# Transposing query rows of two heads as fp32 and splitting them while they leave PSUM

## The chip, the cores and the metric

The kernel runs on one core of one Trainium2 chip. The metric is the device time of one execution in microseconds (us). Five engines matter here: TensorE (PE in the profile; its weight loads are PEld), VectorE (DVE), ScalarE (ACT), GpSimd (POOL) and SyncE (SP), the last two mainly as issuers of DMA transfers.

## The reference, cut to what matters

A decoder trunk of four layers on a sequence of 256 positions with 2048 features, all in fp32. Layers 0 and 3 are latent attention, layer 1 is attention with a selection of keys, layer 2 is attention in a window. Every layer has one input projection, four heads of attention to a memory, a SiLU gate and one output projection. Two places of it concern the change:

```python
# latent attention (layers 0 and 3): 16 heads, a plain part of 128 and a rotary part of 64
q_nope, q_rope = q[..., :A_NOPE], _rope(q[..., A_NOPE:])
s = (einsum('bqhd,bkhd->bhqk', qn, k_nope) + einsum('bqhd,bkd->bhqk', qr, k_rope)) * scale
...
# attention with the selection (layer 1): 32 heads of 64, 4 key heads
q = q.reshape(B, S, B_KV_HEADS, G, B_HEAD_DIM)
s = einsum('bqgjd,bqkgd->bqgjk', qb, kg) * B_HEAD_DIM ** -0.5 + bias
```

## The kernel before, in words

**Precision by two parts.** A product of fp32 accuracy is made from fp32r operands: a value v is split into a high part (v written as fp32r) and a low part (v minus the high part). `split` (lines 67 to 69) does this with a copy on ACT and a subtraction on DVE. The weights are split so, 512 columns at a time, into `wh` and `wl` (`parts_of`, line 234, three buffers of each); then TensorE multiplies high by high, high by low and low by high. `rows_by` (line 240) gives the product with positions on the partitions, `columns_by` (line 270) with features on the partitions; `gate` (line 460) is made of two `columns_by` of 16 steps each.

**Queries of 64 features.** A head with 64 features leaves half of the 128 contraction rows unused, so high and low part are stacked: 64 rows hold the high part and 64 the low part, and the key side holds the same key part in both halves. One pass over the stacked query then gives both products. Which half holds which part doesn't matter, since the key side is the same in both.

**How the stack is made before.** The product has positions on the partitions and must be transposed.
- Rotary queries (`rotary`, line 669; called from `project` for groups 0 and 2 of each latent layer, so four times): for two tiles `t` of 128 positions and two sets `z` of four heads, `rope` (line 592, four DVE instructions) writes `qrr`; `split` (line 678) writes high and low part side by side into `qrs`, of which there is one buffer; `transposed` (line 449) makes four 128x128 transposes in fp32r (line 456), one for each head, into one PSUM tile `tr`, and one ACT copy of 512 columns (line 457, recorded at line 60) into `self.qr`.
- Queries of layers 1 and 2 (`Grouped.project`, line 900; called for four groups in each): `stacked` (line 782) does the same from the accumulator, with an ACT copy that scales (line 787) and a DVE operation that scales and subtracts (line 788), then `transposed`.

So a head is transposed as one 128x128 tile that is half high part and half low part, for each of the two tiles of positions.

**What sets the order.** The kernel is written with a framework that orders each engine's instructions itself from its own estimate of their times (`schedule_with_timeline_sim=True`, line 1201); only what is passed to `keep_in_program_order` stays as written. An engine takes its instructions in that order. While a group's queries are made, the gate of the same group, the attention of the part before and its output projection (`w_out`, line 1113) are at hand for TensorE. PSUM has two kinds of buffers: four "acc" for projections, four "mp" for all else (scores, transposes, attention outputs).

**The order of heads in attention.** In layers 1 and 2 it is 0, 2, 1, 3, 4, 6, 5, 7 (line 917); the first four lie in the tile `q[0]`, the last four in `q[1]`. In latent layers it is 0 to 3 (line 707), all in one tile of `self.qr`.

Of the kernel before, what the change touches and what calls it, by code (L numbers as in the profile page):

```python
# [8 lines left out]
F32 = mybir.dt.float32  # L9
F32R = mybir.dt.float32r  # L10
# [5 lines left out]
P = 128  # L16
S = 256
# [6 lines left out]
A_QL, A_KVL, A_ROPE, A_NOPE = 1536, 512, 64, 128  # L24
# [7 lines left out]
def kernel(ctx: ExitStack, tc: tile.TileContext, a: dict, out: bass.AP,  # L32
                             kinds=(0, 1, 2, 0)):
    nc = tc.nc
# [4 lines left out]
    wk = ctx.enter_context(tc.tile_pool(name="wk", bufs=1))  # L39
# [3 lines left out]
    def misc(name, dt=F32):  # L43
        return ps.tile([P, 512], dt, name=name, tag="mp", bufs=4)
# [8 lines left out]
    def f32(ap):  # L53
        return ap.bitcast(F32)

    def part_tile(dt=F32R):
        return wk.tile([P, 512], dt, name="hl", tag="hl", bufs=2)

    def copy_act(o, i, scale=1.0):
        inst = nc.scalar.activation(o, i, AF.Copy, scale=scale)  # L60
        if pinned:
            tc.keep_in_program_order(inst)
# [4 lines left out]
    def split(hi, lo, src):  # L67
        copy_act(hi, src)
        nc.vector.tensor_sub(lo, src, f32(hi))  # L69
# [22 lines left out]
    ident = cst.tile([P, P], F32, name="ident")  # L92
# [147 lines left out]
    def rows_by(xt, kts, w, k0, cols, name, prepare=None, each=None, late=None):  # L240


        acc = [ps.tile([P, 512], F32, name=f"acc_{name}{t}", tag="acc", bufs=4) for t in range(2)]
        for s in range(0, kts, ST):
            m = min(ST, kts - s)
            wr, n = stage(w, k0 + s, m, cols, each)
            other_work()
            for k in range(m):
                if prepare is not None:
                    prepare(s + k)  # L250
                wh, wl = parts_of(wr, k * n, n)
                q = xt[(s + k) // 4]
                for t in range(2):
                    xh, xl = (q[:, v, (s + k) % 4, t * P:(t + 1) * P] for v in range(2))
                    first, last = s + k == 0, s + k == kts - 1
                    if late is not None and t == 0:

                        both = late[:, s + k].rearrange("p v c -> p (v c)")
                        if not last:
                            nc.tensor.matmul(acc[t][:, :n], both, wh[:, :n], start=first, stop=False)  # L260
                        nc.tensor.matmul(acc[t][:64, :n], both[:, :64], wl[:, :n], start=False, stop=False)
                        if last:
                            nc.tensor.matmul(acc[t][:, :n], both, wh[:, :n], start=False, stop=True)
                        continue
                    nc.tensor.matmul(acc[t][:, :n], xh, wh[:, :n], start=first, stop=False)  # L265
                    nc.tensor.matmul(acc[t][:, :n], xh, wl[:, :n], start=False, stop=False)  # L266
                    nc.tensor.matmul(acc[t][:, :n], xl, wh[:, :n], start=False, stop=last)  # L267
        return acc

    def columns_by(xt, kts, w, k0, cols, name):  # L270

        acc = [ps.tile([P, 2, S], F32, name=f"acc_{name}{j}", tag="acc", bufs=4) for j in range(2)]
        for s in range(0, kts, 2 * ST):
            m = min(2 * ST, kts - s)
            wr, n = stage(w, k0 + s, m, cols)
            other_work()
            for k2 in range(0, m, 2):
                wh, wl = parts_of(wr, k2 * S, 2 * S)
                for k in range(2):
                    kt = s + k2 + k  # L280
                    q = xt[kt // 4]

                    for j in range(2):
                        o = k * S + j * P
                        nc.tensor.matmul(acc[j], wh[:, o:o + P], q[:, :, kt % 4, :],  # L285
                                         start=kt == 0, stop=False)
                    for j in range(2):
                        o = k * S + j * P
                        nc.tensor.matmul(acc[j][:, 0, :], wl[:, o:o + P], q[:, 0, kt % 4, :],  # L289
                                         start=False, stop=kt == kts - 1)  # L290
        return acc

    def total(acc, name="z"):
        z = wk.tile([P, S], F32, name=name, tag="z", bufs=3)
        copy_act(z, acc[:, 1, :])
        nc.vector.tensor_add(z, z, acc[:, 0, :])
        return z
# [151 lines left out]
    def transposed(dst, srcs, c0=0):  # L449


        for i0 in range(0, len(srcs), 4):
            i1 = min(len(srcs), i0 + 4)
            tp = misc("tr", F32R)
            for i in range(i0, i1):
                nc.tensor.transpose(tp[:, (i - i0) * P:(i - i0 + 1) * P], srcs[i], identr)
            copy_act(dst(i0, i1), f32(tp)[:, :(i1 - i0) * P].rearrange("p (j c) -> p j c", c=P)[:, :, c0:])


    def gate(nm, w, c0):  # L460
        gT = act.tile([P, 4, S], F32, name="gT", tag="gT", bufs=2)
        for h in range(2):
            acc = columns_by(nm.at, 16, w, 0, (c0 + h * S, S), "g")
            for j in range(2):
                z = total(acc[j])
                hz = wk.tile([P, S], F32, name="hz", tag="z", bufs=3)
                nc.vector.tensor_mul(hz, z, nm.half)
                th = wk.tile([P, S], F32, name="th", tag="e", bufs=4)
                nc.scalar.activation(th, hz, AF.Tanh)
                nc.vector.scalar_tensor_tensor(gT[:, 2 * h + j, :], th, 1.0, hz, op0=OP.add, op1=OP.mult)  # L470
        return gT
# [120 lines left out]
    def rope(dst, src, t, n):  # L592

        cb = cos[:, t, None, :].to_broadcast([P, n, A_ROPE])
        q = A_ROPE // 2
        rot = wk.tile([P, 4, A_ROPE], F32, name="rot", tag="rot", bufs=1)[:, :n]
        nc.vector.tensor_mul(rot[:, :, :q], src[:, :, q:], sin[:, t, None, :q].to_broadcast([P, n, q]))
        nc.vector.tensor_mul(rot[:, :, q:], src[:, :, :q], sin[:, t, None, q:].to_broadcast([P, n, q]))
        nc.vector.tensor_mul(dst, src, cb)
        nc.vector.tensor_add(dst, dst, rot)  # L600


    class Latent:
# [65 lines left out]
        def rotary(self, g):  # L669

            self.qr = [act.tile([P, 4, S], F32R, name="qrT", tag="aux", bufs=AUX) for z in range(2)]
            acc = rows_by(self.cT[:3], 12, a["w_uq"][self.j], 0, (g * 768, 8, 192, A_NOPE, A_ROPE), "qr")
            for t in range(2):
                for z in range(2):
                    rr = wk.tile([P, 4, A_ROPE], F32, name="qrr", tag="z", bufs=3)
                    rope(rr, acc[t][:, z * S:(z + 1) * S].rearrange("p (h d) -> p h d", h=4), t, 4)
                    rs = wk.tile([P, 4, 2, A_ROPE], F32R, name="qrs", tag="qrs", bufs=1)
                    split(rs[:, :, 0, :], rs[:, :, 1, :], rr)
                    transposed(lambda i0, i1: self.qr[z][:, i0:i1, t * P:(t + 1) * P],
                               [rs[:, h].rearrange("p a b -> p (a b)") for h in range(4)])  # L680

        def project(self, g):

# [50 lines left out]
    class Grouped:  # L734
# [165 lines left out]
        def project(self, g):  # L900
            nm = self.nm
            acc = rows_by(nm.at, 16, self.w, 0, (g * 512, 512), "q")
            q = [act.tile([P, 4, S], F32R, name="qS", tag="pq", bufs=PQ) for z in range(2)]
            for t in range(2):
                self.stacked(lambda i0, i1: q[i0 // 4][:, :, t * P:(t + 1) * P], acc[t],
                             nm.col("eighth", t), 8)
            bm = act.tile([P, 8, S], F32, name="bm", tag="big3")
            tab = tabs[0 if self.sparse else 1][g]
            nc.gpsimd.dma_start(bm, bass.AP(tensor=tab.tensor, offset=tab.offset + 127,
                                            ap=[[8 * N_TAB - 1, P], [N_TAB, 8], [1, S]]))  # L910
            return g, q, bm, gate(nm, self.w, self.g0 + g * 512)
# [189 lines left out]
    nm = Norm(0)  # L1101
# [3 lines left out]
    for i in range(depth):  # L1105
# [33 lines left out]
        else:  # L1139
            w_out(*pending, True)  # L1140
            nxt.finish()
            nm = nxt
# [62 lines left out]
```

## Time and profile before

| | before |
|---|---|
| median of three runs | 2587.08 us (2586.99 to 2587.45) |
| profiled execution | 2586.98 us |
| span in the profile, first to last instruction | 2585.2 us |
| mean granted TensorE clock | 0.999 |
| DMA, over the span | 520.02 MB, mean 201 GB/s |

How to read the rows below. A row of the waits says which engine, line and tile waited for which, with the total in us, the number of times and the longest. A row of the groups has the line, the engine, the operation, output and inputs with their shapes, the count; then busy us and the mean ns of one; then the idle time ahead of it on its engine and what ended it. A row of the timeline has the start and the length in us, the engine, the line and the count of like instructions in a row; a bracket gives idle time and what ended it. Copies and splits are recorded at lines 60 and 69, inside the helpers, so the tiles' names tell them apart: `tr` is the PSUM tile of a transpose, `qrT` the stacked rotary query, `qS` the stacked query of layers 1 and 2, `hl` the pair of parts of `stacked`, `ptp` the transposed attention weights, `x` at line 184 the rows of the residual stream.

### The profile page before, as it was taken

How to read it: one execution, taken by the hardware profiler on the slowest of the kernel's cores; microseconds unless marked ns; L12 is line 12 of the kernel's file. 1: busy time of each engine (PE TensorE's matmuls, PEld its weight loads, DVE VectorE, ACT ScalarE, POOL GpSimd, SP SyncE). 2: the span in 40 equal slices, each digit the busy share in tenths (PEclk: the TensorE clock that was granted, in tenths of full speed). 3: DMA queues.
4: the chain of work that ended last, by engine and by line, in shares of the span. 5: the costliest groups of instructions: out<-in, count | busy, mean ns of one | idle time of the engine just before them, and what ended most of it. 6: DMA issues, size and time to landing. Idle time of an engine off the chain costs nothing. (4 is left out here: it accounts for less than half of the span.)

```text
span 2585.2 us, 41767 instructions
## 1 busy us (share of the span) xinstructions
PE 2573.5 (100%) x14050; PEld 2214.7 (86%) x14050; DVE 1878.4 (73%) x4139; ACT 1622.3 (63%) x3451; POOL 86.8 (3%) x159
## 2 busy tenths in 40 slices
PE   9999999999999999999999999999999999999998
PEld 7888898888888888888888888888888888888887
DVE  6666667676776686877778776777778767777676
ACT  6556556556656566667666666676666655665655
POOL 1000000000000010000000000000000000000000
PEclk9999999999999999999999999999999999999999
DMA  9888777666777667566556575555655877676664
GB/s 305 257 256 268 236 219 229 184 167 195 190 203 202 196 216 247 167 203 189 187 166 199 169 225 171 172 174 185 195 156 147 240 203 198 192 195 180 212 172 179
DMA packets 459417, 520.02 MB, mean 201 GB/s; under 512 B 69521, under 2 KB 353057, under 8 KB 457537
## 3 DMA queue, kind: packets, MB, share of 16 engines
q1 hardware_dynamic: 441744, 449.72, 58.5%
q0 software_dynamic: 16736, 66.65, 8.0%
q8 instruction: 110, 1.80, 0.3%
q14 instruction: 107, 0.87, 0.1%
q10 hardware_dynamic: 720, 0.98, 0.1%
HBM read 494.10 MB, written 35.75 MB: 205 GB/s over the span
## 5 line engine op out<-in xcount | busy, mean ns | idle before, releaser
L69 DVE TENSOR_TENSOR wl<-wr,wh 128x512 fp32r<-128x512 f32 (+2 forms) x1720 | 1161.3, 678 | 619.0 <-ACT wh L60 597.2
L60 ACT ACTIVATE wh<-wr 128x512 fp32r<-128x512 f32 (+2 forms) x1720 | 1066.1, 621 | 800.5 <-PE acc_g L285 170.5
L285 PE MATMUL acc_g<-xT,wh 128*128 128x512 f32 x1536 | 486.7, 396 | 0.0
L289 PEld LDWEIGHTS acc_g<-xT,wl 128*128 128x128 f32 x1536 | 284.5, 188 | 60.5
L289 PE MATMUL acc_g<-xT,wl 128*128 128x256 f32 x1536 | 310.2, 280 | 0.0
L266 PE MATMUL acc_wo<-wl,y 128*128 128x512 f32 x752 | 297.3, 395 | 0.2 <-DVE wl L69 0.2
L267 PE MATMUL acc_wo<-wh,y 128*128 128x512 f32 x752 | 291.8, 390 | 0.0
L285 PEld LDWEIGHTS acc_g<-xT,wh 128*128 128x128 f32 x1536 | 238.3, 189 | 4.5
L265 PE MATMUL acc_wo<-wh,y 128*128 128x512 f32 x752 | 235.7, 392 | 0.2
L266 PEld LDWEIGHTS acc_wo<-wl,y 128*128 128x128 f32 x752 | 141.3, 188 | 27.7 <-DVE wl L69 0.6
L267 PEld LDWEIGHTS acc_wo<-wh,y 128*128 128x128 f32 x752 | 141.3, 188 | 27.3
L265 PEld LDWEIGHTS acc_wo<-wh,y 128*128 128x128 f32 x752 | 139.3, 188 | 28.7 <-ACT y L60 1.0
L285 PE MATMUL acc_mk<-mT,wh 128*128 128x512 f32 x512 | 161.5, 396 | 0.3 <-ACT wh L60 0.3
L285 PE MATMUL acc_mq<-xT,wh 128*128 128x512 f32 x512 | 161.6, 396 | 0.0
L1118 DVE TENSOR_TENSOR x<-x,acc_wo 128x512 f32<-128x512 f32 x184 | 121.1, 682 | 4.4 <-PE acc_wo L267 4.3
L285 PE MATMUL acc_qn<-cT,wh 128*128 128x512 f32 x384 | 121.3, 397 | 0.0
L285 PE MATMUL acc_cq<-xT,wh 128*128 128x512 f32 x384 | 120.9, 396 | 0.0
L289 PEld LDWEIGHTS acc_mk<-mT,wl 128*128 128x128 f32 x512 | 96.1, 188 | 22.8 <-DVE wl L69 0.4
L289 PEld LDWEIGHTS acc_mq<-xT,wl 128*128 128x128 f32 x512 | 93.9, 188 | 20.1
L289 PE MATMUL acc_mq<-xT,wl 128*128 128x256 f32 x512 | 103.1, 282 | 0.0
L266 PE MATMUL acc_q<-wl,xT 128*128 128x512 f32 x256 | 101.2, 395 | 0.0
L289 PE MATMUL acc_mk<-mT,wl 128*128 128x256 f32 x512 | 101.1, 278 | 0.0
(326 smaller groups left out, 4340.6 us busy)
## 6 DMA issues: line engine op xcount, KB each, us to landing
wr<-in_w_out_dram SPq DMA_DIRECT2D x188, 512.0 KB, 3.7
wr<-in_w_in_a_dram SPq DMA_DIRECT2D x176, 512.0 KB, 4.5
wr<-in_w_mem_kv_dram SPq DMA_DIRECT2D x120, 512.0 KB, 4.7
wr<-in_w_in_b_dram SPq DMA_DIRECT2D x112, 512.0 KB, 3.5
wr<-in_w_in_c_dram SPq DMA_DIRECT2D x104, 512.0 KB, 3.6
wr<-in_w_uq_dram SPq DMA_DIRECT2D x192, 128.0 KB, 3.1
wr<-in_w_uq_dram SPq DMA_DIRECT2D x48, 256.0 KB, 3.9
tab<-flat POOLq DMA_DIRECT2D x8, 1536.0 KB, 9.6
```

The costliest lines, as they stand in the source:

```text
L60: inst = nc.scalar.activation(o, i, AF.Copy, scale=scale)
L69: nc.vector.tensor_sub(lo, src, f32(hi))
L265: nc.tensor.matmul(acc[t][:, :n], xh, wh[:, :n], start=first, stop=False)
L266: nc.tensor.matmul(acc[t][:, :n], xh, wl[:, :n], start=False, stop=False)
L267: nc.tensor.matmul(acc[t][:, :n], xl, wh[:, :n], start=False, stop=last)
L285: nc.tensor.matmul(acc[j], wh[:, o:o + P], q[:, :, kt % 4, :], start=kt == 0, stop=False)
L289: nc.tensor.matmul(acc[j][:, 0, :], wl[:, o:o + P], q[:, 0, kt % 4, :], start=False, stop=kt == kts - 1)
L1118: nc.vector.tensor_add(xs, xs, acc[t])
```

## The change

Two heads of 64 are transposed together as one fp32 tile of 128 columns, before the split; the split is made on the way out of PSUM. Of the transposed tile the partitions 0 to 63 hold an even head and 64 to 127 an odd one. For each half, ACT copies it as fp32r to the same partitions of the stacked query (the high part), and DVE subtracts this from PSUM and writes the difference to the other 64 partitions (the low part). For the odd heads high and low part have so changed places. The rotary loop is turned around (`z` outside, `t` inside), since a PSUM tile now takes both tiles of positions of two pairs of heads: four fp32 transposes for a set of four heads, where there were eight. In the layer with the selection ACT writes the scaled rows as plain fp32 into a tile of the "hl" buffers first, 256 columns at a time, and DVE's scaling subtraction goes. The window layer keeps `stacked`.

```diff
+    def four_heads(dst, rows_):
+
+        tp = misc("tr")
+        for t in range(2):
+            for p in range(2):
+                c = (2 * p + t) * P
+                nc.tensor.transpose(tp[:, c:c + P], rows_[t][:, p * P:(p + 1) * P], ident)
+        for h, main, low in ((0, slice(0, 64), slice(64, P)), (1, slice(64, P), slice(0, 64))):
+            feats = tp[main].rearrange("p (j c) -> p j c", j=2)
+            copy_act(dst[main, h::2, :], feats)
+            nc.vector.tensor_sub(dst[low, h::2, :], feats, f32(dst)[main, h::2, :])
...
-            for t in range(2):
-                for z in range(2):
+            for z in range(2):
+                rows_ = []
+                for t in range(2):
                     rr = wk.tile([P, 4, A_ROPE], F32, name="qrr", tag="z", bufs=3)
                     rope(rr, acc[t][:, z * S:(z + 1) * S].rearrange("p (h d) -> p h d", h=4), t, 4)
-                    rs = wk.tile([P, 4, 2, A_ROPE], F32R, name="qrs", tag="qrs", bufs=1)
-                    split(rs[:, :, 0, :], rs[:, :, 1, :], rr)
-                    transposed(lambda i0, i1: self.qr[z][:, i0:i1, t * P:(t + 1) * P],
-                               [rs[:, h].rearrange("p a b -> p (a b)") for h in range(4)])
+                    rows_.append(rr.rearrange("p h d -> p (h d)"))
+                four_heads(self.qr[z], rows_)
...
-            for t in range(2):
-                self.stacked(lambda i0, i1: q[i0 // 4][:, :, t * P:(t + 1) * P], acc[t],
-                             nm.col("eighth", t), 8)
+            if self.sparse:
+                for z in range(2):
+                    rows_ = part_tile(F32)
+                    for t in range(2):
+                        copy_act(rows_[:, t * S:(t + 1) * S], acc[t][:, z * S:(z + 1) * S],
+                                 scale=nm.col("eighth", t))
+                    four_heads(q[z], [rows_[:, t * S:(t + 1) * S] for t in range(2)])
+            else:
+                for t in range(2):
+                    self.stacked(lambda i0, i1: q[i0 // 4][:, :, t * P:(t + 1) * P], acc[t],
+                                 nm.col("eighth", t), 8)
```

## The prediction

> **What bounds the kernel now.** I read the page's first table, then who makes TensorE wait, then the timeline around the changed lines.
>
> ```profile
> PE 2573.5 (100%) x14050; PEld 2214.7 (86%) x14050; DVE 1878.4 (73%) x4139; ACT 1622.3 (63%) x3451; POOL 86.8 (3%) x159
> ```
>
> ```profile
> PE acc_mv L265 <- ACT wh L60: 1.2, 1, 1.2
> PE wu L102 <- DVE ones L98: 1.1, 1, 1.1
> PE o L951 <- DVE pT L69: 0.3, 1, 0.3
> PE acc_mk L285 <- ACT wh L60: 0.3, 1, 0.3
> PE acc_wo L266 <- DVE wl L69: 0.2, 1, 0.2
> ```
>
> The second view gives every wait of TensorE: total us, times, longest. They add up to 3.1 us of a span of 2585.2 us. TensorE's stream of matmuls is the whole length of the kernel; DVE (73%) and ACT (63%) run beside it. A busy share of 100% could still hide pauses, because a record's length includes the drain that overlaps the next one. So below I take **start to start**, which is what a matmul really costs the stream.
>
> A group of four transposes of the kind the change removes (fp32r, line 456), in the rotary part of layer 0. Columns: start, length, engine, line, operation, count.
>
> ```profile
> 557.51 0.63 PE L285 MATMUL acc_g<-xT,wh 128*128 128x512 f32 x2
> 557.98 0.39 PE L289 MATMUL acc_g<-xT,wl 128*128 128x256 f32 x2
> 558.20 0.63 PE L285 MATMUL acc_g<-xT,wh 128*128 128x512 f32 x2
> 558.67 0.46 PE L456 MATMUL tr<-identr,qrs 128*128 128x128 f32 x4
> 558.97 0.47 PE L289 MATMUL acc_g<-xT,wl 128*128 128x256 f32 x2
> 559.28 0.63 PE L285 MATMUL acc_g<-xT,wh 128*128 128x512 f32 x2
> ```
>
> Without transposes the period of four gate matmuls is 558.20 − 557.51 = 0.69 us. With the group inside it is 559.28 − 558.20 = 1.08 us. The group costs 0.39 us: 0.30 to the next start, and the rest on the pair behind it, which takes 0.31 instead of 0.22. Every start is rounded to 0.01, so this difference of two periods may be 0.37 to 0.41. I take 0.37, the end that lies nearer to the next row.
>
> In the layer with the selection the same kind of group comes as eight, right behind an fp32 transpose:
>
> ```profile
> 1204.46 0.27 PE L488 MATMUL ptp<-ident,e 128*128 128x128 f32 x1
> 1204.49 0.87 PE L456 MATMUL tr<-identr,hl 128*128 128x128 f32 x8
> 1205.20 0.47 PE L289 MATMUL acc_g<-xT,wl 128*128 128x256 f32 x2
> 1205.51 0.62 PE L285 MATMUL acc_g<-xT,wh 128*128 128x512 f32 x2
> ```
>
> Eight take 0.71 us. The pair behind them is late as above (0.31), but it would be late behind the L488 transpose as well. So 0.71 / 2 = 0.36 us for a group.
>
> A group of four fp32 transposes, of the kind the change puts in (plain fp32 data, identity `ident`), stands at line 184:
>
> ```profile
> 944.25 0.60 PE L184 MATMUL tp<-ident,x 128*128 128x128 f32 x4
> 944.60 0.70 PE L265 MATMUL acc_wo<-wh,y 128*128 128x512 f32 x2
> 945.14 0.60 PE L184 MATMUL tp<-ident,x 128*128 128x128 f32 x4
> ...
> 946.51 0.63 PE L265 MATMUL acc_wo<-wh,y 128*128 128x512 f32 x2
> 946.97 0.39 PE L266 MATMUL acc_wo<-wl,y 128*128 128x512 f32 x1
> ```
>
> 0.35 us to the next start, then a pair of 0.54 us where the usual pair takes 0.46. **0.43 us a group**: dearer than the fp32r group, by 0.06.
>
> **The change part by part.** How often, and what the other engines do:
>
> ```profile
> L60 ACT ACTIVATE qrT<-tr 128x512 fp32r<-128x512 f32 x16 | 9.5, 591 | 1.8 <-PE tr L456 1.8
> L60 ACT ACTIVATE qS<-tr 128x512 fp32r<-128x512 f32 x32 | 19.0, 593 | 4.1 <-PE tr L456 4.1
> L60 ACT ACTIVATE qrs<-qrr 128x256 fp32r<-128x256 f32 x16 | 6.6, 410 | 0.0
> L69 DVE TENSOR_TENSOR qrs<-qrr,qrs 128x256 fp32r<-128x256 f32 x16 | 6.8, 423 | 2.0 <-ACT qrs L60 1.3
> L788 DVE SCALAR_TENSOR_TENSOR hl<-acc_q,x,hl 128x256 fp32r<-128x256 f32 x32 | 15.4, 480 | 6.1 <-ACT hl L60 5.5 <-PE acc_g L289 0.6
> L836 ACT ACTIVATE lo<-acc_iq 64x512 f32<-64x512 f32 x1 | 0.6, 596 | 0.3 <-PE acc_iq L263 0.3
> L838 DVE TENSOR_TENSOR zq<-lo,acc_iq 64x512 f32<-64x512 f32 x1 | 0.7, 680 | 0.4 <-ACT lo L836 0.4
> ```
>
> One copy out of PSUM follows each group of four, so these rows count the groups. Rotary queries: 16 groups (four calls: groups 0 and 2 of two latent layers, four tiles each). The qS row holds two layers; the one with the selection has half, 16.
>
> *TensorE.* Removed: 16 × 0.37 + 16 × 0.36 = 11.7 us. Added: 8 sites × 2 tiles = 16 groups × 0.43 = 6.9 us, as 64 transposes instead of 128. Net **−4.8 us**, and by the rounding between −4.5 (0.36 for every removed group, 0.44 for every added) and −5.4 (0.41 for the rotary groups). No row shows a transpose of exactly these new tiles, but the operand form (fp32, 128x128, `ident`) is that of line 184.
>
> Here a rule speaks against the change. The Trainium skill, "FP8 and Floating Point Precision", TensorE Precision Notes, says that true fp32 takes four passes through the array. By it the added transposes would take four times the columns, and half as many would cost more than before (+3.0 us by the fourth rival below, where the rows give −4.8). The L184 rows do not agree: 0.35 us for four fp32 transposes against 0.30 us for four fp32r ones.
>
> *ACT.* Rotary: the 16 copies qrs (410 ns) go; 16 copies of 128x512 become 16 of 64x512, and the L836 row shows 596 ns for half the partitions, so they cost the same. −6.6 us. Layer with the selection: four 128x256 and four copies of 512 elements before and after: 0. ACT's gain is worth nothing by itself, since TensorE is the stream.
>
> *DVE.* Each subtraction over 256 elements becomes one over 64x512 (680 ns, L838). Rotary 16 × (0.68 − 0.42) = +4.2 us; selection 16 × (0.68 − 0.48) = +3.2 us. +7.4 us in all, about 1 us at each of eight sites. I cost it at 0. The cover is the idle time of these stretches (columns: stretch, length, PE, PEld, DVE, ACT, POOL busy, clock, DMA):
>
> ```profile
> 550.00:575.00 25.00, 25.00 (x151) 21.91 (x150) 18.56 (x43) 15.10 (x29) 0.00 (x0) 1.00 0.62 179
> 1200.00:1215.00 15.00, 15.00 (x92) 13.09 (x91) 12.27 (x28) 12.51 (x28) 0.92 (x1) 1.00 0.63 211
> ```
>
> The rotary stretch leaves DVE 6.4 us, the selection stretch 2.7 us, against 1 us more. Without the cover the cost would be the whole +7.4 us.
>
> *Order and buffers.* No DMA is added, moved or passed by another. The rotary chain had one `qrs` buffer for four rounds of split, transpose, copy; that is gone. New: a transposed tile is read by ACT, DVE, ACT, DVE rather than by ACT once, so one of four "mp" PSUM buffers is held perhaps 2.6 us (2 × 0.60 + 2 × 0.68, an estimate from the rows above) instead of 0.6. The first score of a group now waits for a subtraction too. Behind a waiting score on TensorE stand gate and output products. I cost this at 0: before, TensorE shows no wait on `tr`, `qrT` or `qS`, and in the layer with the selection even heads, which are finished first, are scored first. From both sides: 0, and up to the price of the slow rival below; nothing below 0, because TensorE does not wait there now. The framework also orders the instructions anew, so pauses elsewhere can come or go: taken as 0, with the ends in the rivals.
>
> Sum: −4.8 us. The profiled execution was 2586.98 us (span 2585.2 and 1.8 around it, which the change does not touch); the median of the three runs is 2587.08, 0.1 above. So 2587.08 − 4.8 = **2582.3 us**.
>
> **The rivals.**
>
> *Faster: the pauses that are left go too.* The later half has a few:
>
> ```profile
> 1446.20 0.64 PE L265 MATMUL acc_wo<-wh,y 128*128 128x512 f32 x2
> 1446.99 0.50 PE L266 MATMUL acc_wo<-wl,y 128*128 128x512 f32 x1 [0.15 <-DVE wl L69]
> ...
> 1447.79 0.39 PE L267 MATMUL acc_wo<-wh,y 128*128 128x512 f32 x1
> 1448.26 0.50 PE L265 MATMUL acc_wo<-wh,y 128*128 128x512 f32 x1
> ```
>
> ```profile
> 1929.34 0.39 PE L951 MATMUL o<-pT,vz 128*128 128x512 f32 x1
> 1930.07 1.10 PE L951 MATMUL o<-pT,vz 128*128 128x512 f32 x5 [0.34 <-DVE pT L69]
> ```
>
> Against usual starts of 0.46, 0.23 and 0.23 us they lose 0.33, 0.24 and 0.50, together 1.1 us. With a new order they may vanish: 2582.3 − 1.1 = 2581.2 us. For it: the first two sit in the layer that changes. Against it: they are the end of attention, not the queries.
>
> *Slower: ACT stands behind DVE between the two copies of a tile.* Both halves write interleaved rows of one tile. If the second copy is made to wait for the first subtraction, ACT stops for the subtraction that DVE has in front (a `wl` of 512 elements, priced as L838, 0.68) and for the one it waits for (0.68): 1.36 us. Behind it on ACT are the `wh` copies that feed TensorE. What ACT has in hand at each step is shown in brackets:
>
> ```profile
> 561.35 0.63 ACT L60 ACTIVATE wh<-wr 128x512 fp32r<-128x512 f32 x1 [0.70 <-PE acc_g L285]
> ```
>
> 1.36 − 0.70 = 0.66 us lost at 16 places, 10.6 us: 2582.3 + 10.6 = 2592.9 us. It decides from 4.8 / 16 = 0.30 us a place. Against it: three `wh` buffers stand between ACT and TensorE, and the bracket says that ACT waits for TensorE, not the other way.
>
> *DVE becomes the bound at the sites:* the whole +7.4 us, 2582.3 + 7.4 = 2589.7 us. Against it: the stretches above.
>
> *Four passes for fp32:* a 128-column transpose priced as a 512-column matmul (0.23 us): 64 × 0.23 = 14.7 us added against 11.7 us removed, +3.0: 2590.1 us. The L184 rows speak against it. The Trainium skill, "FP8 and Floating Point Precision", TensorE Precision Notes, has the rule.
>
> **How the numbers follow.** A kernel of this length can hardly be told from no change within 0.2%, 5.2 us: 2581.9 to 2592.3. My forecast has 0.48, the fast rival 0.24, the slow one 0.20, DVE as the bound 0.06, four passes 0.02. The forecast alone goes from 2581.7 to 2582.6 by its bounds; about a quarter of its 0.48, so 0.12, lies below 2581.9. Faster 0.24 + 0.12 = 0.36; slower 0.20; within 0.36 + 0.08 = 0.44. The range goes from 2580.0 (the fast rival on the −5.4 bound, with a pause more) to 2592.0, just short of the slow rival.
>
> **What would show it.** Right: L456 loses 128 transposes, 64 fp32 ones of 0.35 us for four appear; the starts around them show 0.43 us a group; the busy sum of PE falls by about 5 us; TensorE's waits stay near 3 us; ACT falls by 6.6 us and DVE grows by 7.4. Wrong: a wait of TensorE on `wh`, `wl`, `qS` or `qrT`; an ACT copy of the second half released by DVE; pauses in start to start far from the edit, where only the order changed; or a group of fp32 transposes that takes near 0.9 us.

## The result and the profile after

| | before | changed |
|---|---|---|
| median of 22 runs | 2586.97 us (2586.25 to 2589.24) | 2582.81 us (2581.80 to 2585.18) |
| ratio, with its 95% interval | | 0.9984 (0.9978 to 0.9990) |
| span of the profiled execution | 2585.2 us | 2581.7 us |

The change takes off 4.2 us, or 0.16%. The predicted time was 2582.3 us. In what follows "the changed kernel" is the one with the whole change, and its line numbers are its own: line 467 is a transpose of `four_heads`, 471 its subtraction, 502 the transposes `ptp`, 580 the memory scores `msp`, 972 and 978 the attention output `o` and its product with the gate, `yt`.

First the page of the changed kernel, its table of busy times:

```profile
PE 2569.7 (100%) x13986; PEld 2210.8 (86%) x13986; DVE 1885.5 (73%) x4139; ACT 1618.6 (63%) x3435; POOL 87.1 (3%) x159
```

TensorE has 64 matmuls fewer (14050 before) and is busy 3.8 us less, where about 5 was looked for; VectorE is busy 7.1 us more (7.4 was worked out); ScalarE has 16 instructions fewer. TensorE is still the length of the kernel. The view of its waits says that nothing new holds it up for long:

```profile
PE acc_mv L265 <- ACT wh L60: 1.3, 2, 1.1
PE wu L102 <- DVE ones L98: 1.1, 1, 1.1
PE o L972 <- DVE ms L583: 0.3, 1, 0.3
PE msp L580 <- DMA mkr<-mkT: 0.2, 1, 0.2
PE acc_wo L266 <- DVE wl L69: 0.2, 1, 0.2
```

No `qrT`, no `qS`, no `tr`. One row is new, `msp` waiting for keys that a DMA brings; it comes back below. The timeline of the same gate as before, with the new transposes in it:

```profile
557.42 0.63 PE L285 MATMUL acc_g<-xT,wh 128*128 128x512 f32 x2
557.89 0.38 PE L467 MATMUL tr<-ident,qrr 128*128 128x128 f32 x2
...
558.34 0.62 PE L285 MATMUL acc_g<-xT,wh 128*128 128x512 f32 x2
...
559.04 0.63 PE L285 MATMUL acc_g<-xT,wh 128*128 128x512 f32 x2
```

A period with a pair of fp32 transposes takes 558.34 − 557.42 = 0.92 us, one without 559.04 − 558.34 = 0.70. The pair costs 0.22, four cost 0.44; the forecast took 0.43. In the layer with the selection the transposes of a group of heads come as eight:

```profile
1203.35 1.04 PE L467 MATMUL tr<-ident,hl 128*128 128x128 f32 x8
1204.14 0.48 PE L289 MATMUL acc_g<-xT,wl 128*128 128x256 f32 x2
```

0.79 us to the next start, so 0.40 for four, a little under 0.43. (The pair behind is late here as it was before the change, so it is left out of both.) The groups of the changed kernel show what ScalarE and VectorE now do at a site, and what ended the idle time ahead of it (behind the bar):

```profile
L471 DVE TENSOR_TENSOR qrT<-tr,qrT 64x512 fp32r<-64x512 f32 x16 | 11.0, 689 | 2.2 <-ACT qrT L60 1.8
...
L60 ACT ACTIVATE qrT<-tr 64x512 fp32r<-64x512 f32 x16 | 9.4, 588 | 3.3 <-PE tr L467 2.4 <-DVE qrT L471 0.9
L60 ACT ACTIVATE qS<-tr 64x512 fp32r<-64x512 f32 x16 | 8.8, 587 | 3.2 <-PE tr L467 3.1
```

The subtraction takes 0.69 us (0.68 was taken) and the copy of half the partitions 0.59, as much as that of all of them. The last column has the slow rival's wait, one of the prediction's signs of being wrong: ScalarE stands idle 0.9 us for the subtraction `qrT`. The view of ScalarE's waits has no more of it in the whole kernel.

**Where the time came off.** The transposes at line 184 are the same in both kernels, so they serve as landmarks. From the timelines, first of before (its row at 944.25 is in the prediction), then of the changed kernel; the last row of each is its last matmul:

```profile
401.49 0.60 PE L184 MATMUL tp<-ident,ckv 128*128 128x128 f32 x4
...
1499.08 1.03 PE L184 MATMUL tp<-ident,x 128*128 128x128 f32 x8
...
2020.13 0.60 PE L184 MATMUL tp<-ident,ckv 128*128 128x128 f32 x4
...
2576.46 0.28 PE L985 MATMUL acc_wo<-wk,y 128*128 128x256 f32 x1
```

```profile
402.10 0.60 PE L184 MATMUL tp<-ident,ckv 128*128 128x128 f32 x4
...
943.67 0.60 PE L184 MATMUL tp<-ident,x 128*128 128x128 f32 x4
...
1496.18 1.03 PE L184 MATMUL tp<-ident,x 128*128 128x128 f32 x8
...
2017.63 0.60 PE L184 MATMUL tp<-ident,ckv 128*128 128x128 f32 x4
...
2572.79 0.28 PE L1006 MATMUL acc_wo<-wk,y 128*128 128x256 f32 x1
```

The differences of two starts are the stretches:

| stretch | sites of the change | before | changed | difference |
|---|---|---|---|---|
| start-up, to the first landmark | none | 401.49 | 402.10 | +0.61 |
| layer 0 | two rotary calls | 542.76 | 541.57 | −1.19 |
| layer 1, selection | four groups | 554.83 | 552.51 | −2.32 |
| layer 2, window | none | 521.05 | 521.45 | +0.40 |
| layer 3 | two rotary calls | 556.33 | 555.16 | −1.17 |

The eight sites give 4.68 us, 0.6 us each: the forecast's 4.8. Two stretches without a site give 1.0 back in this execution. The 0.61 of the start-up is chance between executions: in another execution of the same kernel (the first experiment) the first landmark is at 401.44. The 0.40 of the window layer is the new wait:

```profile
1531.68 0.63 PE L285 MATMUL acc_mq<-xT,wh 128*128 128x512 f32 x2
1532.56 0.71 PE L580 MATMUL msp<-mkr,mqT 128*128 128x256 f32 x4 [0.24 <-DMA mkr<-mkT]
```

The next start comes 0.88 us after a pair that takes 0.46 elsewhere, because the keys of the memory haven't landed when the shorter stream asks for them (tested below, "Keys first").

### The profile page after: what moved, and what is told of

Its sections match the earlier page's. It is cut to its first block, busy times and chain, and to the rows that moved or that the text cites. A ratio compares the mean times of both kernels' runs of the same rounds, so it can differ in the third digit from the quotient of the medians.

```text
span 2581.7 us, 41595 instructions
## 1 busy us (share of the span) xinstructions
PE 2569.7 (100%) x13986; PEld 2210.8 (86%) x13986; DVE 1885.5 (73%) x4139; ACT 1618.6 (63%) x3435; POOL 87.1 (3%) x159
```

## The experiments

The theory: TensorE's stream alone counts. A group of four transposes costs it 0.36 or 0.37 us in fp32r and 0.43 in fp32, and VectorE's added work, and the turn-taking of the two engines on a tile, lie under other work. The rivals: the saving is due to something else (the type, the lost `qrs` round); or VectorE and ScalarE are covered here only by luck of place, and the price shows as soon as the same form stands elsewhere.

All runs were timed in five rounds, 11 times each, against the kernel before on the same chip: 2587.10 us beside the first four of the table, 2587.06 beside the next four, 2586.94 beside the last four. Stretches are between the landmarks above, in us.

| kernel | median | against before | layer 0 | layer 1 | layer 2 |
|---|---|---|---|---|---|
| the change again | 2582.92 | −4.18, 0.9984 (0.9975 to 0.9993) | 541.58 | 552.52 | 521.38 |
| rotary alone | 2584.63 | −2.47, 0.9990 (0.9981 to 0.9999) | 541.57 | 554.85 | 520.97 |
| selection alone | 2585.01 | −2.09, 0.9992 (0.9984 to 1.0001) | 542.73 | 552.52 | 521.59 |
| window layer too | 2587.97 | +0.87, 1.0003 (0.9994 to 1.0011) | 541.57 | 552.55 | 526.21 |
| fp32, same count | 2588.82 | +1.76, 1.0007 (0.9999 to 1.0016) | 543.31 | 555.50 | 520.93 |
| subtracted twice | 2590.99 | +3.93, 1.0015 (1.0006 to 1.0024) | 541.94 | 560.19 | 520.89 |
| keys first | 2582.64 | −4.42, 0.9983 (0.9974 to 0.9992) | 541.58 | 552.55 | 520.90 |
| window, half of it | 2588.68 | +1.62, 1.0006 (0.9997 to 1.0015) | 541.58 | 552.55 | 527.16 |
| window busier | 2587.10 | +0.16, 1.0000 (0.9991 to 1.0009) | 541.60 | 552.51 | 525.92 |
| copies first | 2584.66 | −2.28, 0.9991 (0.9982 to 1.0000) | 541.58 | 554.44 | 520.93 |
| copies first, window too | 2590.13 | +3.19, 1.0012 (1.0003 to 1.0021) | 541.57 | 554.42 | 526.45 |
| copies and keys first | 2584.21 | −2.73, 0.9990 (0.9981 to 0.9998) | 541.58 | 554.58 | 520.94 |

**The change again.** No edit.

> The changed kernel itself, to have it on the same chip as its parts. Theory (TensorE's stream gets shorter by 0.6 us at each of eight places and nothing else moves): 4.2 to 4.8 us under the kernel before. Rival (part of the difference is chance in the first 30 us or in a transfer): the difference leaves this interval, and the profile shows it in TensorE's waits of the first 100 us.

−4.18 us: the gain is there again, and each layer takes what it took in the first execution, to 0.07 us.

**Rotary alone.**

```diff
-            if self.sparse:
+            if False:
```

> Only the rotary queries are changed; the layer with the selection keeps its transposes of split tiles. Theory: 16 x 0.37 - 8 x 0.43 = 2.5 us under the kernel before, and the starts of TensorE's rows after each of four rotary places are 0.6 us earlier. Rival (the gain comes from a new order of the whole program): no fixed share, anything from 0 to 4.8 us.

−2.47 us; layer 0 is as in the changed kernel, layer 1 as before.

**Selection alone.** The rotary loop is that of before, with `split`, `qrs` and `transposed`.

> Only the layer with the selection is changed; rotary queries keep their split ahead of the transpose. Theory: 16 x 0.36 - 8 x 0.43 = 2.3 us under the kernel before, and with the rotary part alone it adds up to the whole change. Rival (a new order): the two parts don't add up to the whole within 1 us.

−2.09 us, layer 1 shorter by 2.31, and the pause ahead of the memory scores is there (521.59 in layer 2). The two parts together give 4.56 us, the whole 4.18: they add up within what such runs can tell apart, and neither needs the other.

**The type alone: fp32, same count.** The kernel before, with the same 128 transposes made in fp32.

```diff
-            tp = misc("tr", F32R)
+            tp = misc("tr", F32 if plain else F32R)
...
-                nc.tensor.transpose(tp[:, (i - i0) * P:(i - i0 + 1) * P], srcs[i], identr)
+                nc.tensor.transpose(tp[:, (i - i0) * P:(i - i0 + 1) * P],
+                                    f32(srcs[i]) if plain else srcs[i], ident if plain else identr)
...
```

> The kernel before, with its 128 transposes of split tiles at the changed places made as fp32 instead of fp32r: the kind of the change without its smaller number. Theory (a group of four fp32 transposes takes 0.43 us where fp32r takes 0.36 to 0.37): 32 x 0.065 = 2.1 us over the kernel before. Rival (fp32 goes through the array in four passes): 128 x 0.23 - 11.7 = 17.7 us over it.

The view of one line, with shortest, median and longest record in ns, for the transposes of this kernel:

```profile
L456 PE MATMUL tr<-identr,hl x120: 218/236/304, 988.4 to 1853.2; 128*128 128x128 f32 x120
L456 PE MATMUL tr<-ident,qrs x64: 271/272/275, 560.0 to 2371.4; 128*128 128x128 f32 x64
```

+1.76 us over 32 groups, 0.055 us a group: about the 0.06 of the forecast. The interval of the whole time just includes no change, but every stretch with such transposes is longer: 0.55 us in layer 0, 0.67 in layer 1. So it is the halved count that pays, and the type takes a part of it back. Four passes, as the prediction priced them, would have cost ten times as much. The rule of the Trainium skill that the prediction weighed ("FP8 and Floating Point Precision", TensorE Precision Notes) does not give the price of these 128x128 transposes.

**Window layer too.** The same form in the layer that kept `stacked`.

```diff
-            if self.sparse:
+            if True:
```

> The change, and the window layer's queries in the same way. Theory: another 16 x 0.36 - 8 x 0.43 = 2.3 us, so about 6.9 us under the kernel before and 2.3 under the changed one. Rival (DVE's longer subtractions are not hidden where that layer already pauses for DVE): at most 1 us under the changed kernel, with new waits of TensorE on wl, pT or qS in the third layer.

The theory fell. In layer 2 sixteen more fp32r groups are gone for eight of fp32, and the time is 5.05 us above the changed kernel of the same runs; 4.8 of it is lost in layer 2. Its timeline:

```profile
1695.50 0.69 DVE L471 TENSOR_TENSOR qS<-tr,qS 64x512 fp32r<-64x512 f32 x1
...
1696.95 0.69 DVE L471 TENSOR_TENSOR qS<-tr,qS 64x512 fp32r<-64x512 f32 x1
1697.67 0.69 DVE L978 TENSOR_TENSOR yt<-o,gT 128x512 f32<-128x512 f32 x1
1698.20 0.63 ACT L60 ACTIVATE wh<-wr 128x512 fp32r<-128x512 f32 x1 [2.33 <-PE acc_wo L267]
1698.73 0.61 ACT L60 ACTIVATE y<-yt 128x512 fp32r<-128x512 f32 x1
1699.40 0.50 PE L265 MATMUL acc_wo<-wh,y 128*128 128x512 f32 x1 [1.24 <-ACT y L60]
```

Two of the new subtractions stand ahead of `yt` on VectorE. In the changed kernel `yt` of this place starts at 1695.48, here at 1697.67. ScalarE's copy of it, `y`, can't start before `yt` ends at 1698.36. It starts at 1698.73, as a `wh` copy, which waited 2.33 us for TensorE to set a buffer free, stands ahead of it: at most 0.37 us of the delay is that copy's. TensorE, whose next matmul is the output product, stops 1.24 us for `y`. The same happens behind 1855.6 us. The layer's other new stops are shorter, 0.5 us twice for `pT` and once for `wh` the longest of them.

**Window, half of it.** There the first four heads keep `stacked`, the second four are made by `four_heads`.

> The change, and in the window layer only the second set of four heads, whose scores come later, is transposed as fp32 pairs; the first set keeps its split ahead. Theory (in the window layer it was two subtractions just ahead of the gated product that stopped TensorE; half of them, for heads needed later, leave room): 0.5 to 1.2 us under the changed kernel. Rival (any subtraction out of PSUM at that place stops TensorE): over the changed kernel, with waits on y or pT in the third layer.

5.8 us above the changed kernel by the gains of the table, no better. The wait of the slow rival shows in the timeline:

```profile
1697.29 0.59 ACT L60 ACTIVATE qS<-tr 64x512 fp32r<-64x512 f32 x1 [0.16 <-DVE qS L471]
1697.94 0.63 ACT L60 ACTIVATE wh<-wr 128x512 fp32r<-128x512 f32 x1
...
1698.63 0.73 PE L265 MATMUL acc_wo<-wh,y 128*128 128x512 f32 x2 [0.78 <-ACT wh L60]
```

ScalarE's second copy is released by the first subtraction, the `wh` copy comes behind it, and TensorE waits 0.78 us for that. But ScalarE was idle only 0.16 us for the subtraction, so at most that much of the stop is the rival's. Most of what TensorE waits for in this layer is something else, and not the `y` or `pT` that were expected:

```profile
PE acc_g L285 <- DVE z L296: 2.2, 3, 1.1
...
PE acc_wo L265 <- DVE z L296: 1.2, 2, 0.6
```

Line 296 is the addition with which VectorE empties a PSUM buffer of the projections. TensorE waits 3.4 us for it, so here too VectorE comes late, but at another place.

**Subtracted twice.** The changed kernel with each subtraction of `four_heads` made twice, to the same result: 22 us more on VectorE.

```diff
             nc.vector.tensor_sub(dst[low, h::2, :], feats, f32(dst)[main, h::2, :])
+            nc.vector.tensor_sub(dst[low, h::2, :], feats, f32(dst)[main, h::2, :])
```

> The change with each subtraction out of PSUM done twice, 32 x 0.69 = 22 us more on DVE. Theory (DVE's idle time at these places covers its work): within 1 us of the changed kernel. Rival (the place in DVE's queue decides, as in the window layer, where subtractions stood ahead of the gated product): 3 to 12 us over the changed kernel, with waits of TensorE on y, pT or wl in the second layer.

+8.1 us over the changed kernel, as the rival had it: 0.36 in layer 0 for 5.5 us of added work, but 7.7 in layer 1 for 11. TensorE's waits:

```profile
PE acc_wo L265 <- DVE z L296: 1.4, 3, 0.5
...
PE acc_wo L265 <- ACT y L60: 1.0, 3, 0.3
PE sp L947 <- DVE qS L472: 0.5, 3, 0.2
```

The cover is real beside a rotary call. In layer 1 it was enough for the change, and for no more than about 3 of the 11 us beyond it.

**Window busier.** The changed kernel, whose window layer keeps `stacked`, with the scaling subtraction there issued twice: 7.7 us more on VectorE, and the old order.

> The changed kernel, whose window layer keeps its old way (copy, scaling subtraction, eight fp32r transposes, one copy of each), but the scaling subtraction there is issued twice, to the same result: 16 more operations of 0.48 us, 7.7 us of VectorE, 1.9 us a group. The four-head form gives VectorE less than that, 16 x 0.2 = 3.2 us. If the window layer lost 5 us under the new form because VectorE has no 3 us to spare there, this kernel loses as much or more: 2587 to 2591 us. If the loss is in the form itself (ScalarE standing behind a subtraction between its two copies, or the subtractions that now follow the transposes and stand ahead of the split of the attention outputs), the added work ahead of the transposes costs little: 2582.8 to 2584 us.

2587.10 us, 4.3 above the changed kernel by the gains of the table, and layer 2 is 4.5 us longer than with the change alone (525.92 against 521.38 and 521.45). So VectorE's time is dear in this layer in whatever form. Its timeline at the place of the window experiment's stop:

```profile
1695.49 0.63 ACT L60 ACTIVATE y<-yt 128x512 fp32r<-128x512 f32 x1 [0.24 <-DVE yt L979]
...
1696.17 0.50 PE L265 MATMUL acc_wo<-wh,y 128*128 128x512 f32 x1 [0.53 <-ACT y L60]
```

TensorE stops at the same product, for the same chain of `yt` and `y`. About 0.6 us is lost here for each us of VectorE that is added. By that rate (an estimate, which takes the loss to grow evenly) the 3.3 us that `four_heads` adds in the window layer (16 × (0.69 − 0.48)) would cost 2 us, about what it saves the stream; but the layer became 4.8 us longer. So VectorE's time alone hardly explains the loss. That the order in which the new work stands carries the rest is likely, but no run shows it by itself.

**Copies first.** In the kernels above the new form takes a tile out by copy, subtraction, copy, subtraction, and the second copy waits for the first subtraction. Here both copies are issued first; ScalarE's second copy then waits for nothing of VectorE.

```diff
+        halves = [(h, main, low, tp[main].rearrange("p (j c) -> p j c", j=2))
...
+        for h, main, low, feats in halves:
             copy_act(dst[main, h::2, :], feats)
+        for h, main, low, feats in halves:
             nc.vector.tensor_sub(dst[low, h::2, :], feats, f32(dst)[main, h::2, :])
```

> The changed kernel with the two ScalarE copies of a transposed tile issued before the two VectorE subtractions, instead of copy, subtraction, copy, subtraction. ScalarE's second copy then waits for nothing of VectorE. The same work, the same count. If the wait between the copies is covered at the eight sites, as the milestones of the changed kernel say (0.57 to 0.6 us gained a site of a possible 0.6), nothing changes: 2582.8 within 0.6 us. If it holds up ScalarE where the profile shows 0.9 us idle ahead of the rotary copies, about that comes back: 2582 us. Slower by more than 1 us only if a subtraction that is now later holds up the scores: then a wait of TensorE on qS or qrT of VectorE.

It took a wait away and lost 1.9 us (554.44 against 552.51 in layer 1), though not by a wait on `qS` or `qrT`, the one way to be slower that was expected. VectorE's timeline of the changed kernel at the first group, then that of this kernel with TensorE's row:

```profile
1113.83 0.69 DVE L471 TENSOR_TENSOR qS<-tr,qS 64x512 fp32r<-64x512 f32 x1
1114.54 0.69 DVE L69 TENSOR_TENSOR wl<-wr,wh 128x512 fp32r<-128x512 f32 x1
1115.27 0.70 DVE L471 TENSOR_TENSOR qS<-tr,qS 64x512 fp32r<-64x512 f32 x1
```

```profile
1115.13 1.39 DVE L473 TENSOR_TENSOR qS<-tr,qS 64x512 fp32r<-64x512 f32 x2
1116.55 1.29 DVE L69 TENSOR_TENSOR wl<-wr,wh 128x512 fp32r<-128x512 f32 x2
1117.30 0.39 PE L289 MATMUL acc_g<-xT,wl 128*128 128x256 f32 x1 [0.56 <-DVE wl L69]
```

In the changed kernel subtractions and weight splits take turns, the first `wl` at 1114.54. Without the wait the subtractions come in pairs, the first `wl` starts at 1116.55, and the gate stops 0.56 us for it. That is the only new stop of layer 1 that the view of waits names; the rest of the 1.9 us lies in shorter pauses, which were not traced to a cause.

**Copies first, window too.**

> The four-head form in the window layer as well (which took 2588.0 us, 5 us over the changed kernel), with both copies ahead of both subtractions. If ScalarE's second copy standing behind the first subtraction is what the window layer pays for, the 5 us come back, and with them the gain of 16 groups of transposes less, 16 x 0.36 - 8 x 0.43 = 2.3 us: 2580.5 us, with 2581 to 2583 if half does. If the subtractions themselves are the matter (four of 0.69 us in a row on VectorE, ahead of the split of the attention outputs on which the output products wait), it stays at 2587 to 2589 us, with TensorE's waits on y, wl and wh as there.

Layer 2 takes 526.45 us, against 526.21 with the wait between the copies: the wait is not what the window layer pays for. (The time is above the 2587 to 2589 us of that case by about the 1.9 us that this order loses in layer 1.) What stands there instead, in its timeline:

```profile
1693.95 2.40 ACT L60 ACTIVATE qS<-tr 64x512 fp32r<-64x512 f32 x4
1695.16 2.81 DVE L473 TENSOR_TENSOR qS<-tr,qS 64x512 fp32r<-64x512 f32 x4 [0.22 <-ACT qS L60]
1696.38 0.49 ACT L60 ACTIVATE pT<-ptp 128x384 fp32r<-128x384 f32 x1
1696.92 0.50 PE L974 MATMUL o<-pT,vz 128*128 128x512 f32 x1 [0.73 <-ACT pT L60]
```

Four copies in one block keep ScalarE 2.40 us from `pT`, four subtractions keep VectorE 2.81 us. TensorE's stops have mostly moved, from `y` to `pT` and `wh`.

**Keys first.** The changed kernel with the memory's keys loaded ahead of its values, since the values are wanted later.

```diff
-        for z in range(2):
-            pin(nc.gpsimd.dma_start(v[z], mv[i][part][:, z]))
...
+            if h == 0:
+                for z in range(2):
+                    pin(nc.gpsimd.dma_start(v[z], mv[i][part][:, z]))
```

> The change, and the first keys of the memory are loaded ahead of the memory's values in each memory part. Theory (the new wait of TensorE on mkr at 1532 us, 0.3 to 0.5 us, comes from a transfer that lands a little late now that TensorE arrives earlier): that wait goes, 0.3 to 0.5 us under the changed kernel. Rival (the wait is chance of one execution): no difference.

The wait is gone from the waits, and the memory scores follow 0.47 us after the start of a pair, without a pause (timeline):

```profile
1530.56 0.63 PE L285 MATMUL acc_mq<-xT,wh 128*128 128x512 f32 x2
1531.03 0.63 PE L581 MATMUL msp<-mkr,mqT 128*128 128x256 f32 x4
```

Layer 2 is back at 520.90 us. The time, 2582.64 us, is 0.2 us under the changed kernel's, less than the runs can tell apart.

**Copies and keys first.** Both edits.

> The changed kernel with both copies ahead of both subtractions, and the memory's keys loaded ahead of its values. The keys' order took away the pause of 0.4 us ahead of the memory scores at 1532 us, and 0.2 to 0.3 us of the time. With the copies' order costing or giving nothing: 2582.5 us. With a part of ScalarE's idle time ahead of the second copies given back too: 2582.0 us or less.

2584.21 us, where at most 2582.5 was expected. The copies' order costs in layer 1 what it cost alone; layer 2 has no pause in either.

## Why the prediction was right

**The stream.** Forecast −4.8 us from eight sites, measured −4.68 between landmarks. The prices stood: four fp32 transposes 0.44 at rotary sites and 0.40 in the layer with the selection (0.43), fp32 over fp32r 0.055 (0.06). The parts run alone agree with the split: −2.47 and −2.09 us, and in their stretches −1.19 in layer 0 and −2.31 in layer 1.

**VectorE's 7.4 us costed at nothing.** It cost nothing (7.1 us on the page), but the reason given was too weak for layer 1. The forecast set the idle time of a stretch, 2.7 us, against 1 us of new work. Subtracted twice, a group adds about 2.7 us more and loses 1.9 of it. The same sum, with VectorE's work at nothing, was off by 7 us in the window layer (2.3 us gained was expected, 4.8 were lost). So that layer 1 had room was in part luck: the prediction did not ask which products of the stream stood behind the new work in VectorE's queue. Beside rotary calls the argument held.

**ScalarE's 6.6 us worth nothing.** The rows of `qrs` are gone; the page's total falls by 3.7 only. It counts records that overlap once: the groups' own times add up to 1773 us before, the page has 1622.3. No gain came from it that the stream doesn't explain.

**Order and buffers costed at nothing.** Right at the sites. Elsewhere one new pause of 0.4 us came (the memory's keys), a case of the prediction's "pauses elsewhere can come or go". With it the sum is −4.68 + 0.40 = −4.28, beside the measured −4.16; the rest is within the spread of the start-up.

**The fast rival.** The pauses that it hoped to see go are all there. The last of them, in the changed kernel's timeline:

```profile
1926.94 0.39 PE L972 MATMUL o<-pT,vz 128*128 128x512 f32 x1
1927.67 1.09 PE L972 MATMUL o<-pT,vz 128*128 128x512 f32 x5 [0.34 <-DVE ms L583]
```

0.73 us from start to start at this one, to the hundredth what it was before; the two at the end of layer 1 are as long as they were, too.

**The other rivals.** The slow one: its mechanism is there, the second copy does wait for the first subtraction, but ScalarE is idle for it for 0.9 us in the whole changed kernel, where the rival had 0.66 us lost at each of 16 places, and none of it reaches TensorE. In the window layer, half changed, it is at most 0.16 of a stop of 0.78 us. Its remedy, copies first, made things worse: at the first group of layer 1 the wait keeps the two engines' work in turns. VectorE as the bound at the sites is refuted for the change, and true in layer 1 for the doubled subtractions. Four passes are refuted.

**What stays open.** Why layer 1 has room for the form and layer 2 has not. The windows of the changed kernel over the groups of layer 1 and of layer 2 (stretch, length, PE, PEld, DVE, ACT, POOL busy, clock, DMA):

```profile
1090.00:1480.00 390.00, 389.78 (x2074) 332.27 (x2073) 309.79 (x726) 260.96 (x585) 9.44 (x13) 1.00 0.60 188
1680.00:1960.00 280.00, 279.58 (x1507) 237.63 (x1506) 216.11 (x526) 189.78 (x455) 3.80 (x5) 1.00 0.56 175
```

VectorE is busy 79% of the first and 77% of the second, so the share does not tell. The stops show places: the chain from `o` by `yt` and `y` to the output product above all, and the emptying of PSUM buffers (`z`) where half was changed. But no run moved the output product away from that chain. Nor was it settled why the framework makes the second copy wait.

## What to carry to other kernels

Where one engine's stream is the kernel, count its instructions start to start; here the sum held to some tenths of a us. Work put on another engine was hidden here not by that engine's idle share but by what stands behind it in its queue: find the next instruction that the stream is waiting for, and ask whether the new work comes ahead of it. A wait that makes engines take turns may be worth keeping, so try the removal before you trust it, and don't carry a gain from one layer to the next without a look at that layer's own queue.

## What the runs showed of the hardware

A copy or subtraction over 64 partitions takes as long as one over 128: 0.59 us for 64x512 and for 128x512 on ScalarE (`tr` to `qrT` and `qS`), 0.69 us for both on VectorE (`qrT`, `yt`). An fp32 transpose of 128x128 shows 272 ns a record where fp32r shows 236, and 0.055 us more for four in the stream. The stretch ahead of the first landmark, which none of the edits but the keys' touches, took from 401.32 to 402.81 us in these executions, more than some of the differences that the experiments looked for. Stretches between landmarks were steadier: layer 0 took 541.57 to 541.60 us in all ten executions with the new rotary form and single subtractions.
